# A two-layer trunk: the first stage in a written order with four column groups, two of them summed in SBUF, and the bias of pw2 as products

## The chip, the cores and the metric

The kernel runs on one core of a Trainium2 chip. The metric is the device time of one execution in microseconds; the number given for the kernel before is the median of three runs.

## The reference, cut to what matters

The trunk has two layers on 256 tokens of width 2048, all in float32. Layer 0 mixes tokens by a Conformer convolution, layer 1 by differential attention; both end in a squared-ReLU MLP of width 8192. Each sub-layer is modulated by vectors made from a condition `c`. The change lies in layer 0's mixer:

```python
cond = jax.nn.silu(c)
mod = cond @ ada_w[i] + ada_b[i]                       # [2048] x [2048, 12288]
sh_m, sc_m, g_m, sh_f, sc_f, g_f = jnp.split(mod, 6, axis=-1)
h = x * (1.0 + sc_m) + sh_m
# conformer_conv(h)
u = h @ w1 + b1                                        # pw1: [256, 2048] x [2048, 4096]
a, gt = jnp.split(u, 2, axis=-1)
u = a * sigmoid(gt)
u = depthwise_conv31(u) + b_dw                         # causal, per channel
u = silu(layer_norm(u, g, b))
y = u @ w2 + b2                                        # pw2: [256, 2048] x [2048, 2048]
x = layer_norm(alpha * x + g_m * y, ln_mix_g, ln_mix_b)
h = x * (1.0 + sc_f) + sh_f                            # the MLP follows
```

## The kernel before, in words

**Products.** A float32 product is made of three: weights and activations are each split into a rounded part (hi) and the rest (lo), and hi·hi, hi·lo and lo·hi are added up in PSUM. A weight tile comes by DMA in halves or whole (512 KB to 1 MiB), ACT casts it to hi (L424, later L493), DVE (later sometimes POOL) subtracts to get lo (L426, L494), and PE runs the products, 128 rows of k, 128 tokens and 512 columns each (L440 to L442 in pw1, L526 to L528 in pw2). There are two token tiles.

**Condition vectors.** `cond` is the SiLU of c, made on ACT (L156) and DVE, and copied 32 times for PE (L160). A slice of a modulation vector is made in one of two ways from 1 MiB loads `aw`. `ada_slice_dve_steps`: DVE multiplies each row block by its cond column and sums up (L236), and at the end PE adds over partitions with a vector of ones (L218). `ada_slice_steps`: PE multiplies with the copied cond (L268), ACT copies the row out (L272), PE transposes it (L253), and DVE adds the bias. In names such as `aw_3_8_1` the first number is the vector (0 SH_M, 1 SC_M, 2 G_M, 3 SH_F, 4 SC_F), the second its first block of 128 columns, the third the load; `aacc`, `aps`, `arow` and `apt` are the sums, the PE sums, the row and the columns of such a slice.

**The first stage** (loop at L850 to L880). pw1 has eight column groups of 256 + 256 columns (value and gate). While the shift and scale of the first sub-layer are still coming in, in four slices of 512 features, three groups, 2, 0 and 1 (`FIRST`), are multiplied slice by slice, as far as h is known. Their six accumulators (three groups, two token tiles) take all four banks `mm` and two of the three banks `tp` that transposes use too. Raw ada loads use the two buffers `araw` and, two in three, the four weight buffers `wraw`. In this stage a scheduler that simulates the engines sets the order of each engine's instructions; from its end PE's order is as written.

**The rest of layer 0's mixer.** Groups 3 to 7 follow, 16 k-blocks each at a stretch (`group`, L446). After each pair of k-blocks a tick passes, and work that was put off by a number of ticks (`defer`) is written there: gating (`glu`, L756 to L783: ACT copies the accumulator out, L760; PE transposes, L773 and L774; sigmoid on ACT; product on DVE), then the convolution (`conv_pe`, L712: taps on DVE, L720; twelve shifted copies on ACT, L729, and four on DVE; 64 small products in each of two halves, L738). `pump_conv` starts steps of the list `ada_q` in between, 32 (`ADA_T1`) by the end of pw1: 16 of G_M, 8 of SC_F and 8 of SH_F. At tick 28 the gate vector is broadcast, and POOL multiplies the bias of pw2 with it and adds it to z (`base_bias`, L659 and L663). Then comes `FILL`: 3, 2, 2, 1 and 0 further ada steps around the last two convolution halves, the LayerNorm and the first transposes of SiLU (`sw`). Then pw2 (`out_proj`, `run_jobs`), four column groups of 512, with the remaining ada steps of layer 0 spread over it (`pump_t2`), and the MLP.

**Small rows.** Biases and gains come as rows by DMA on ACT's queue (L127, L153), are transposed by PE and kept as columns. Some are loaded at the start; `ada_b` of layer 1, the MLP's biases, the gain of the attention's norm and six LayerNorm rows are loaded in `other_vectors`, which stands in the third slice of the first stage. Each of these loads has a completion counter of a small set that both SP's and ACT's loads take in turn, and a load that takes a counter again waits for the load that had it.

## Time and profile before

| | us |
|---|---|
| median of three runs | 2433.89 (2429.94 to 2435.54) |
| the profiled execution, its own time | 2432.41 |
| its span in the trace | 2430.6 |
| PE busy, share of the span | 2277.4, 94% |
| DVE, ACT, POOL busy | 1759.5, 1070.6, 264.9 |

Engines: PE multiplies, PEld loads its weights beside that, DVE, ACT and POOL do elementwise work, SP starts transfers; ACTq and SPq are the queues from which ACT and SP start them. Times are microseconds from the start of the span unless a column says ns. A group's row ends with the idle time of its engine just ahead of it and what ended that. In a window's row stand its length, the busy time and count of each engine, the granted TensorE clock (1 is full), the share of time in which the DMA engines were busy, and the rate.

### The profile page before, as it was taken

What the parts mean: (1) busy time and instruction counts of PE and PEld (TensorE: products, weight loads), DVE (VectorE), ACT (ScalarE), POOL (GpSimd) and SP (SyncE); (2) the same over time, 40 slices, a digit from 0 to 9 for tenths busy, and PEclk for the clock granted to TensorE, in tenths of its full rate; (3) what the DMA queues carried; (4) which work ended last, traced back from release to release, by engine and by line L of the source; (5) the groups of instructions that cost most, each with busy time, mean ns of one, the idle gap of its engine ahead of it and who ended that gap; (6) DMA issues with size and microseconds to landing.
All of it is one profiled execution on the core that took longest, in us unless ns stands there. A gap on an engine that the chain in (4) does not pass through costs nothing.

```text
span 2430.6 us, 28467 instructions
## 1 busy us (share of the span) xinstructions
PE 2277.4 (94%) x11119; PEld 1816.0 (75%) x11119; DVE 1759.5 (72%) x1977; ACT 1070.6 (44%) x1391; POOL 264.9 (11%) x174
## 2 busy tenths in 40 slices
PE   4588997989999999999998999998999999999997
PEld 2366664867778888888876888886788888888886
DVE  5588744879798888878868777886867565565566
ACT  2337554444434434434444544443543443443442
POOL 0000011232150000000024200012214000000002
PEclk9789998999999999999999999999999999999999
DMA  9998767658988888888875666685676555556562
GB/s 354 312 331 292 247 220 263 240 209 290 333 309 319 293 322 278 315 314 294 299 254 189 203 237 220 236 291 185 236 277 227 190 186 190 191 185 197 181 223 102
DMA packets 272547, 609.57 MB, mean 251 GB/s; under 512 B 11098, under 2 KB 44448, under 8 KB 259100
## 3 DMA queue, kind: packets, MB, share of 16 engines
q1 hardware_dynamic: 271560, 607.24, 72.2%
q8 instruction: 87, 1.43, 0.2%
q10 hardware_dynamic: 852, 0.51, 0.1%
q14 instruction: 48, 0.39, 0.0%
HBM read 605.58 MB, written 2.13 MB: 250 GB/s over the span
## 4 chain that ended last, share of the span: by engine, by line
PE 75%; DVE 10%; DMA 6%; ACT 4%; issue 3%; POOL 1%; ACTq 0%; DVEq 0%; SPq 0%; POOLq 0%
PE w_ps L527 17%; PE w_ps L526 17%; PE w_ps L528 17%; DMA aw<-in_ada_w_dram 4%; DVE wl_w L494 2%; DVE aacc L236 2%; PE aps L268 1%; PE pw_ps L440 1%; DVE acc L294 1%; PE pw_ps L441 1%; PE qkv_q_ps L528 1%; PE pw_ps L442 1%; PE qkv_v_ps L528 1%; PE qkv_v_ps L526 1%; PE qkv_v_ps L527 1%
## 5 line engine op out<-in xcount | busy, mean ns | idle before, releaser
L494 DVE TENSOR_TENSOR wl_w<-w_w,wh_w 128x1024 fp32r<-128x1024 f32 x502 | 634.3, 1281 | 332.7 <-ACT wh_w L493 332.5
L493 ACT CAST wh_w<-w_w 128x1024 fp32r<-128x1024 f32 x512 | 537.5, 1053 | 754.1 <-PE w_ps L528 579.3
L526 PE MATMUL w_ps<-wh_w,hm_hi 128*128 128x512 f32 x1024 | 403.9, 394 | 4.5 <-ACT hm_hi L361 4.5
L527 PE MATMUL w_ps<-wl_w,u_hi 128*128 128x512 f32 x1024 | 399.0, 390 | 6.3 <-DVE wl_w L494 6.3
L527 PE MATMUL w_ps<-wl_w,hm_hi 128*128 128x512 f32 x1024 | 400.5, 391 | 4.7 <-DVE wl_w L494 4.7
L528 PE MATMUL w_ps<-wh_w,hm_lo 128*128 128x512 f32 x1024 | 400.8, 391 | 1.0 <-DVE hm_lo L364 1.0
L526 PE MATMUL w_ps<-wh_w,u_hi 128*128 128x512 f32 x1024 | 400.0, 391 | 0.0
L528 PE MATMUL w_ps<-wh_w,u_lo 128*128 128x512 f32 x1024 | 398.6, 389 | 0.0
L294 DVE SCALAR_TENSOR_TENSOR acc<-adaw,cond,acc 128x2048 f32<-128x2048 f32 (+1 forms) x105 | 243.0, 2315 | 0.1
L526 PEld LDWEIGHTS w_ps<-wh_w,hm_hi 128*128 128x128 f32 x1024 | 193.2, 189 | 49.2 <-ACT hm_hi L361 6.2
L527 PEld LDWEIGHTS w_ps<-wl_w,u_hi 128*128 128x128 f32 x1024 | 192.3, 188 | 47.9 <-DVE wl_w L494 8.4
L527 PEld LDWEIGHTS w_ps<-wl_w,hm_hi 128*128 128x128 f32 x1024 | 193.5, 189 | 45.1 <-DVE wl_w L494 6.0
L528 PEld LDWEIGHTS w_ps<-wh_w,hm_lo 128*128 128x128 f32 x1024 | 193.2, 189 | 43.0 <-DVE hm_lo L364 2.6
L526 PEld LDWEIGHTS w_ps<-wh_w,u_hi 128*128 128x128 f32 x1024 | 192.3, 188 | 42.0 <-issue 2.5
L528 PEld LDWEIGHTS w_ps<-wh_w,u_lo 128*128 128x128 f32 x1024 | 192.2, 188 | 39.9
L494 POOL TENSOR_TENSOR wl_w<-w_w,wh_w 128x1024 fp32r<-128x1024 f32 x10 | 24.0, 2404 | 1095.7 <-ACT wh_w L493 1095.7
L236 DVE SCALAR_TENSOR_TENSOR aacc<-aw,cond,aacc 128x512 f32<-128x512 f32 (+1 forms) x120 | 128.2, 1069 | 16.0 <-DMA aw<-in_ada_w_dram 14.0
L426 DVE TENSOR_TENSOR wl_pw<-w_pw,wh_pw 128x1024 fp32r<-128x1024 f32 x64 | 79.8, 1260 | 60.5 <-ACT wh_pw L424 60.4
L440 PE MATMUL pw_ps<-wh_pw,h_hi 128*128 128x512 f32 x256 | 106.6, 416 | 6.2 <-ACT h_hi L361 6.2
L441 PE MATMUL pw_ps<-wl_pw,h_hi 128*128 128x512 f32 x256 | 102.7, 401 | 0.0
L442 PE MATMUL pw_ps<-wh_pw,h_lo 128*128 128x512 f32 x256 | 99.1, 396 | 0.0
L424 ACT CAST wh_pw<-w_pw 128x1024 fp32r<-128x1024 f32 x64 | 65.9, 1048 | 68.6 <-PE pw_ps L442 58.7
(322 smaller groups left out, 3189.4 us busy)
## 6 DMA issues: line engine op xcount, KB each, us to landing
w_w<-in_mlp_w_dram SPq DMA_DIRECT2D x256, 1024.0 KB, 5.5
adaw<-in_ada_w_dram SPq DMA_DIRECT2D x96, 1024.0 KB, 6.1
aw<-in_ada_w_dram SPq DMA_DIRECT2D x84, 1024.0 KB, 7.3
w_pw<-in_conv_pw_w_dram SPq DMA_DIRECT2D x64, 512.0 KB, 7.2
w_pw<-in_conv_pw_w_dram SPq DMA_DIRECT2D x16, 1024.0 KB, 5.2
w_qkv_q<-in_attn_qkv_w_dram SPq DMA_DIRECT2D x16, 1024.0 KB, 5.3
w_qkv_k<-in_attn_qkv_w_dram SPq DMA_DIRECT2D x16, 1024.0 KB, 5.1
w_qkv_v<-in_attn_qkv_w_dram SPq DMA_DIRECT2D x16, 1024.0 KB, 5.2
```

What stands on the lines that cost most here:

```text
L236: nc.vector.scalar_tensor_tensor(st["acc"], wv[:, kc % per, :], cond[:, kc:kc + 1], st["acc"], ALU.mult, ALU.add)
L294: nc.vector.scalar_tensor_tensor(st["acc"], w, cond[:, kc:kc + 1], st["acc"], ALU.mult, ALU.add)
L424: nc.scalar.copy(hi, rq)
L426: eng.tensor_tensor(lo, rq, hi.bitcast(F32), op=ALU.subtract)
L440: nc.tensor.matmul(pss[t], lhsT=xh, rhs=wh, start=(kc == 0), stop=False)
L441: nc.tensor.matmul(pss[t], lhsT=xh, rhs=wl, start=False, stop=False)
L442: nc.tensor.matmul(pss[t], lhsT=xl, rhs=wh, start=False, stop=(kc == nk - 1))
L493: nc.scalar.copy(hi, rq)
L494: eng.tensor_tensor(lo, rq, hi.bitcast(F32), op=ALU.subtract)
L526: nc.tensor.matmul(pss[tt], lhsT=xh, rhs=wh, start=(kc == 0), stop=False)
L527: nc.tensor.matmul(pss[tt], lhsT=xh, rhs=wl, start=False, stop=False)
L528: nc.tensor.matmul(pss[tt], lhsT=xl, rhs=wh, start=False, stop=(kc == nk - 1))
```

## The change

1. **Small rows.** The ten row loads of `other_vectors` move to the start of the program, on ACT's queue, ahead of `cond`.
2. **First stage.** Five slices of 2, 4, 4, 4 and 2 blocks of 128 features. Groups 0 and 1 (`RES`) keep their accumulators in PSUM; groups 2 and 3 (`ROT`) are multiplied into `tp` banks slice by slice, and each slice's result is added to sums in SBUF (first copied by ACT, then added by DVE). Four groups are so done by the end of the stage, in place of three. Raw ada loads use the two `araw` buffers and two halves of the buffer of the convolution, so that the four weight buffers hold weights alone. Loads, splits, ada steps and products of PE, DVE, ACT and SP stand in the order in which they are written (`first_part`).
3. **Convolutions.** `conv_pe` is cut into taps, shifts and products, which are put off to ticks of their own (`CONV_AT`); the taps' 64 small copies become 16.
4. **Steps of ada.** The list is cut in two, `dve_q` (G_M, SC_F) and `pe_q` (SH_F). During pw1 24 steps of `dve_q` run and none of `pe_q`; FILL takes eight of `pe_q`, and pw2 the other eight, with eight of `dve_q`. The gate's broadcast moves from tick 28 into FILL.
5. **Bias of pw2.** `base_bias` goes from here. Each accumulator of pw2 begins with two products with four rows of weights (L549 of the new kernel): a selector of the quarter and the bias, hi and lo.

```diff
-FIRST = (2, 0, 1)
-ADA_T1 = 32
+RES = (0, 1)
+ROT = (2, 3)
+SLICES = ((0, 2), (2, 4), (6, 4), (10, 4), (14, 2))
+ADA_T1 = 24
-SLICES = ((0, 4), (4, 4), (8, 4), (12, 4))
-CONV_AT = {2: 1, 0: 4, 1: 7}
+CONV_AT = (3, 7, 11, 15, 19, 23, 28)
...
+    late_rows = {}
+    for n, (name, vs) in enumerate((("adab1", [ada_b[1]]), ("b1", [mlp_b1[0], mlp_b1[1]]), ("subg", [attn_subln_g[0]]),
+                                    ("ln", [ln_mix_g[0], ln_mix_b[0], ln_ffn_g[0], ln_ffn_b[0], ln_mix_g[1],
+                                            ln_mix_b[1]]))):
+        o = 0
+        for v in vs:
+            r = vec_rows(v)
+            nc.scalar.dma_start(vtok[o:o + r.shape[0], 1, n * P:(n + 1) * P], r)
+            o += r.shape[0]
+        late_rows[name] = vtok[:o, 1, n * P:(n + 1) * P]
     cT = as_cols(c_rows, "c")
...
-        if first and n_raw[0] % 3:
-            return wraw.tile([P, 2048], F32, tag="raw", name=name)
+        if first:
+            n_raw[0] += 1
+            if n_raw[0] % 4 in (3, 0):
+                return ux[:, n_raw[0] % 4 // 3 * 2048:(n_raw[0] % 4 // 3 + 1) * 2048]
         return araw.tile([P, 2048], F32, tag="araw", name=name)
...
+                        if kc == 0 and job["bias"] is not None:
+                            for n, (sel, row) in enumerate(job["bias"]()):
+                                nc.tensor.matmul(pss[tt], lhsT=sel, rhs=row, start=(n == 0), stop=False)
...
+    def ada_pair(s):
+        sc_step, sh_step = ada_step[s].pop(0)
+        sc_step()
+        sh_step()
+        for _ in range(2):
+            if ada_load:
+                ada_load.pop(0)()
...
+    for _ in range(4):
+        ada_load.pop(0)()
+    for t in range(NT):
+        nc.sync.dma_start(z[:, t, :], x[0, t * P:(t + 1) * P, :])
+    for _ in range(N_RAW):
+        load_w()
...
+        for n, g in enumerate(order[s]):
+            split_w()
+            pss = pss0[g] if g in RES else [tp_tile(f"pw1_{g}_{s}_ps{t}") for t in range(NT)]
...
+                mm_parts(pss, hT, parts[:nf // 2], f0, k0, k1, False)
+                end_ada(s + 1)
+                mm_parts(pss, hT, parts[nf // 2:], f0 + nf // 2, k0, k1, False)
...
+            if g in ROT:
+                for t in range(NT):
+                    if s == 0:
+                        nc.scalar.copy(accs[g][t], pss[t])
+                    else:
+                        nc.vector.tensor_tensor(accs[g][t], accs[g][t], pss[t], op=ALU.add)
+                cs[g]["ut"] = accs[g]
```

**ACT, the start of the program.** Before, the load of the activation table and the sigmoid of `cond` stand after the rows that the first stage needs at once, and seven others behind them. A wait `DMAHW6` is one for completion counter 6.

```order
L127 DMA rows_conv<-in_conv_ln_b_dram 16x128 [waits DMAHW3_49]
L156 ACT_TABLE_LOAD
L156 ACTIVATE cond<-cols_c 128x16 [waits DVE_49]
L127 DMA rows_adab_635<-in_ada_b_dram 96x128 [waits DMAHW5_49,PE_49]
L127 DMA rows_ln<-in_ln_mix_g_dram 16x128 [waits DMAHW7_49,PE_49]
L127 DMA rows_ln<-in_ln_mix_b_dram 16x128 [waits DMAHW1_49]
L127 DMA rows_ln<-in_ln_ffn_g_dram 16x128 [waits DMAHW2_49]
L127 DMA rows_ln<-in_ln_ffn_b_dram 16x128 [waits DMAHW3_49]
L127 DMA rows_ln<-in_ln_mix_g_dram 16x128 [waits DMAHW4_49]
L127 DMA rows_ln<-in_ln_mix_b_dram 16x128 [waits DMAHW6_49]
```

Now, with the table and the sigmoid on L165:

```order
L160 DMA vtok<-in_ada_b_dram 96x128 [waits DMAHW5_49]
L160 DMA vtok<-in_mlp_b_dram 64x128 [waits DMAHW7_49]
L160 DMA vtok<-in_mlp_b_dram 64x128 [waits DMAHW1_49]
L160 DMA vtok<-in_attn_subln_g_dram 2x128 [waits DMAHW3_49]
L160 DMA vtok<-in_ln_mix_g_dram 16x128 [waits DMAHW5_49]
L160 DMA vtok<-in_ln_mix_b_dram 16x128 [waits DMAHW7_49]
L160 DMA vtok<-in_ln_ffn_g_dram 16x128 [waits DMAHW1_49]
L160 DMA vtok<-in_ln_ffn_b_dram 16x128 [waits DMAHW3_49]
L160 DMA vtok<-in_ln_mix_g_dram 16x128 [waits DMAHW5_49]
L160 DMA vtok<-in_ln_mix_b_dram 16x128 [waits DMAHW6_49]
L165 ACT_TABLE_LOAD
L165 ACTIVATE cond<-cols_c 128x16 [waits DVE_49]
```

The ten loads stand ahead of the sigmoid. The last of them takes a counter of SP's, as the last one before did; counted through, it is that of SP's twelfth load, 7.25 MiB into what SP asks for.

**DVE, the end of the first stage.** `aacc_1_12` is the last scale slice before, `aacc_2_0` the first slice of G_M; the `wl` are splits of pw1 weights, with group and slice in the name (`wl_pw_1_2`).

```order
L236 SCALAR_TENSOR_TENSOR aacc_1_12_828<-aw_1_12_3_845,cond,aacc_1_12_828 128x512 x2
L364 TENSOR_TENSOR h_lo<-h_h_706,h_hi 128x512
L236 SCALAR_TENSOR_TENSOR aacc_1_12_828<-aw_1_12_3_845,cond,aacc_1_12_828 128x512 x2
L383 TENSOR_SCALAR h_h_716<-h_t_711,h_mul,mod_0_132 128x256
L234 TENSOR_SCALAR aacc_2_0_1106<-aw_2_0_0_1104,cond 128x1024
L236 SCALAR_TENSOR_TENSOR aacc_2_0_1106<-aw_2_0_0_1104,cond,aacc_2_0_1106 128x1024
```

Now the last scale slice is `aacc_1_14`, its second load in half of the convolution's buffer (`conv_ux`):

```order
L249 SCALAR_TENSOR_TENSOR aacc_1_14_955<-conv_ux,cond,aacc_1_14_955 128x256
L249 SCALAR_TENSOR_TENSOR aacc_2_0_1269<-aw_2_0_1_1272,cond,aacc_2_0_1269 128x1024
L249 SCALAR_TENSOR_TENSOR aacc_1_14_955<-conv_ux,cond,aacc_1_14_955 128x256
L249 SCALAR_TENSOR_TENSOR aacc_2_0_1269<-aw_2_0_1_1272,cond,aacc_2_0_1269 128x1024
L249 SCALAR_TENSOR_TENSOR aacc_1_14_955<-conv_ux,cond,aacc_1_14_955 128x256 x3
L249 SCALAR_TENSOR_TENSOR aacc_2_0_1269<-aw_2_0_2_1345,cond,aacc_2_0_1269 128x1024
L249 SCALAR_TENSOR_TENSOR aacc_1_14_955<-conv_ux,cond,aacc_1_14_955 128x256
L447 TENSOR_TENSOR wl_pw_1_3_0_1029<-w_pw_1_3_789,wh_pw_1_3_0_1028 128x1024
L447 TENSOR_TENSOR wl_pw_1_3_1_1033<-w_pw_1_3_789,wh_pw_1_3_1_1032 128x1024
L934 TENSOR_TENSOR vtok<-vtok,pw_3_3_ps_1039 128x512
L934 TENSOR_TENSOR vtok<-vtok,pw_3_3_ps_1040 128x512
L447 TENSOR_TENSOR wl_pw_0_4_0_1068<-w_pw_0_4_840,wh_pw_0_4_0_1067 128x1024
```

Sums of G_M stood behind the last scale sum and now stand between its parts; splits of the fourth slice and the PSUM adds stand behind both.

**PE, around the start of pw2.** `aps_3` are SH_F steps, `cv` and `vt` the last convolutions, `sw` the transposes ahead of SiLU, `pw_0_ps` the first accumulators of pw2.

```order
L738 MATMUL cv_2993<-conv_x,conv_w_1_1_2891 32x256 x16
L268 MATMUL aps_3_12_2981<-aw_3_12_1_3028,condr 32x512 x4
L704 MATMUL vt_3034<-ident,vpe_3026 128x128 x2
L268 MATMUL aps_3_12_2981<-aw_3_12_2_3040,condr 32x512 x4
L268 MATMUL aps_3_12_2981<-aw_3_12_3_3062,condr 32x512 x4
L934 MATMUL sw_3072<-ident,vtok 128x128 x4
L934 MATMUL sw_3082<-ident,vtok 128x128 x4
L934 MATMUL sw_3092<-ident,vtok 128x128 x4
L526 MATMUL pw_0_ps_3112<-wh_pw_0_0_0_3116,swish_hi 128x512
L527 MATMUL pw_0_ps_3112<-wl_pw_0_0_0_3117,swish_hi 128x512
```

Now:

```order
L1031 MATMUL sw_3008<-ident,vtok 128x128 x4
L1031 MATMUL sw_3018<-ident,vtok 128x128 x4
L1031 MATMUL sw_3028<-ident,vtok 128x128 x4
L283 MATMUL aps_3_8_3067<-aw_3_8_0_3065,condr 32x512 x4
L549 MATMUL pw_0_ps_3048<-pw2b_hl,one_2680 128x512 x2
L550 MATMUL pw_0_ps_3048<-wh_pw_0_0_0_3052,swish_hi 128x512
L552 MATMUL pw_0_ps_3048<-wl_pw_0_0_0_3053,swish_hi 128x512
L553 MATMUL pw_0_ps_3048<-wh_pw_0_0_0_3052,swish_lo 128x512
L549 MATMUL pw_0_ps_3049<-pw2b_hl,one_2680 128x512 x2
```

All SH_F steps stood ahead of the first product of pw2; now the first step of its third slice (`aps_3_8`) stands just ahead of it, the other seven of the last two slices stand between products of pw2, and the two bias products open each accumulator.

421 lines of the change are left out of this document (234 added, 187 removed).

## The prediction

> **What bounds the kernel now.** I read the page first, for the whole.
>
> ```profile
> span 2430.6 us, 28467 instructions
> PE 2277.4 (94%) x11119; PEld 1816.0 (75%) x11119; DVE 1759.5 (72%) x1977; ACT 1070.6 (44%) x1391; POOL 264.9 (11%) x174
> PE 75%; DVE 10%; DMA 6%; ACT 4%; issue 3%; POOL 1%; ACTq 0%; DVEq 0%; SPq 0%; POOLq 0%
> ```
>
> PE is busy for 94% of the span and holds 75% of the chain that ended last. The change touches the program up to the end of pw2, so I cut that part into four stretches by the PE rows and asked for the busy time of each engine in them: A, the first stage with three column groups (0 to 185.3); B, the other five groups (to 388.3); C, the last convolutions and the LayerNorm (to 420.6); D, pw2 (to 517.5). Three shorter windows follow. Columns: length, busy time of PE, PEld, DVE, ACT and POOL, granted clock, DMA share, GB/s.
>
> ```profile
> 0.00:185.30 185.30, 115.84 (x523) 77.14 (x523) 116.19 (x197) 57.67 (x100) 1.98 (x11) 0.84 0.96 333
> 185.30:388.30 203.00, 190.45 (x1576) 133.60 (x1574) 133.16 (x182) 119.22 (x179) 17.48 (x12) 0.98 0.73 253
> 388.30:420.60 32.30, 22.32 (x214) 9.17 (x212) 11.25 (x27) 14.89 (x26) 0.72 (x1) 0.84 0.75 261
> 420.60:517.50 96.90, 94.60 (x424) 77.91 (x424) 76.97 (x74) 42.35 (x50) 23.60 (x9) 0.96 0.73 252
> 25.00:50.00 25.00, 14.19 (x54) 6.41 (x47) 9.64 (x14) 8.94 (x13) 0.00 (x0) 0.86 1.07 372
> 100.00:125.00 25.00, 23.33 (x104) 16.58 (x102) 10.51 (x13) 10.31 (x13) 0.00 (x0) 0.84 0.77 250
> 411.70:418.50 6.80, 6.09 (x27) 2.70 (x28) 2.44 (x6) 4.47 (x6) 0.06 (x1) 0.50 0.75 261
> ```
>
> A is bound by transfers: the DMA engines are busy for 0.96 of it, PE for 116 of 185 us. B and D are bound by PE (190 of 203, 95 of 97). So work that moves from B into A's idle PE time is a gain, if A doesn't get longer by as much. Two of the groups on PE up to 192 us say the same, with their idle time and its releaser at the end:
>
> ```profile
> L268 PE MATMUL aps<-aw,condr 128*32 128x512 f32 x128 | 24.9, 887 | 27.0 <-DMA aw<-in_ada_w_dram 27.0
> L218 PE MATMUL apt<-ones,aacc 128*128 128x1 f32 x32 | 4.9, 269 | 14.4 <-DVE aacc L236 14.4
> ```
>
> PE waits 27.0 us for ada weights, and 14.4 us for the DVE sums made from them.
>
> **Stretch A, its start.** The ACT timeline of the first 28 us (start, duration):
>
> ```profile
> 8.14 1.28 ACT L156 ACT_TABLE_LOAD   x1 [8.14 <-DMA rows_adab<-in_ada_b_dram]
> 9.44 0.22 ACT L156 ACTIVATE cond<-cols_c 128x16 f32<-128x16 f32 x1
> 26.09 0.32 ACTq L127 DMA_DIRECT2D rows_ln<-in_ln_mix_b_dram  x1
> 26.44 1.28 ACT L905 ACT_TABLE_LOAD   x1 [16.78 <-DMA z<-in_x_dram]
> ```
>
> The DVE timeline has the copy of cond for PE, behind which the ada steps start:
>
> ```profile
> 9.95 0.42 DVE L160 COPY condr<-cond 128x512 f32<-128x512 f32 x1
> ```
>
> cond is ready at 9.66 now, and both its forms 0.71 later, at 10.37. The last row load goes out only at 26.09, though it is small: the queue's completion counters are shared with SP's loads, and the order lists for it a wait on counter 6, whose earlier user lands then (the page puts the wait of the next ACT instruction down to z). About 7 MiB had been asked for ahead of it. In the new order ten row loads stand ahead of cond, and the last of them waits on counter 6 as well, for SP's twelfth load, which ends 7.25 MiB into the stream. I put it at 27, and both forms of cond at 27 + 0.32 + 1.28 + 0.22 + 0.71 = 29.5 in place of 10.4. The Trainium skill (DMA: Bandwidth & Descriptors, Issuing engines are not separate DMA queues) says that DMAs started by several engines end on the same 16 DMA engines, and that only the sequencer's time to initiate is at stake, usually a small one. By that, ten loads would cost ACT ten issues, cond would come near 14, and A would be about 5 us shorter than I say; the trace disagrees, as the row at 26.09 is an issue of 0.32 us that stood until then.
>
> What a late cond costs is small, since the loads run on until their buffers are full: 4 MiB of ada weights, 2 of x, four weight tiles of 0.5, 8 MiB, full at about 28. The first ada steps give buffers back from 31.5 (PE) to 33.5 (DVE, whose step has eight sums at 0.476, below). So transfers stand still for some 5 us, and resume at 33.5.
>
> **A, its transfers.** From there 40 MiB remain to the last ada load: 32 of ada, 2 of x and 14 of weights make 48, less the 8. One MiB (1.049 MB) takes 2.82 us at the 372 GB/s of the window 25 to 50, and 3.02 at 333 / 0.96 = 347, A's rate while busy. With 2.95, the last ada load lands at 33.5 + 118 = 151.5. In the trace of before (a row below) the last ada step of A starts at 157.6, with one group fewer.
>
> **A, its tail.** DVE and ACT rows by shape (up to 440 us) for this and the rest, then the landing time of a load on a light queue, the last number of its row:
>
> ```profile
> L236 DVE SCALAR_TENSOR_TENSOR aacc<-aw,cond,aacc 128x1024 f32<-128x1024 f32 x48 | 61.4, 1280 | 10.7 <-DMA aw<-in_ada_w_dram 10.3
> L426 DVE TENSOR_TENSOR wl_pw<-w_pw,wh_pw 128x1024 fp32r<-128x1024 f32 x64 | 79.8, 1260 | 60.5 <-ACT wh_pw L424 60.4
> L671 DVE TENSOR_TENSOR pw_g<-pw_ps,gb 128x512 f32<-128x512 f32 x7 | 4.8, 680 | 2.7 <-PE pw_ps L528 2.7
> L783 DVE SCALAR_TENSOR_TENSOR u<-pa,cols_conv,sg 128x256 f32<-128x256 f32 x10 | 4.3, 476 | 2.2 <-ACT sg L781 2.2
> L383 DVE TENSOR_SCALAR h_h<-h_t,h_mul,mod 128x256 f32<-128x256 f32 x8 | 4.2, 538 | 2.6 <-PE h_t L377 2.6
> ```
>
> ```profile
> L729 ACT COPY conv_x<-u 32x568 f32<-32x568 f32 x56 | 37.2, 664 | 8.7 <-DVE u L783 8.0
> L361 ACT CAST h_hi<-h_h 128x512 fp32r<-128x512 f32 x8 | 4.8, 618 | 0.2
> ```
>
> ```profile
> w_w<-in_mlp_w_dram SPq DMA_DIRECT2D x256, 1024.0 KB, 5.5
> ```
>
> In DVE's new order the sums of G_M, a vector that nobody needs before FILL, alternate with those of the last scale slice, up to the third G_M load, which needs the buffer of the first. So the last scale sum waits for: two G_M loads still queued, 2 x 2.95 = 5.9; the step on the first, 2.9; the third load from issue to landing, 5.5; its step and a sum of 0.48, together 1.7: 16.0. (A price of 0 is the other end: R1.) Then, in DVE's order, two splits 2 x 1.26, two PSUM adds 2 x 0.68 (by L671, the row that reads PSUM and SBUF at this width), a split 1.26, three G_M sums of 1.28, small ones 0.7, the h scaling 0.54 and the cast 0.62: 10.8, say 11. The last slice's products come next; PE's timeline gives their pace, and the last ada step of A:
>
> ```profile
> 60.06 0.39 PE L440 MATMUL pw_ps<-wh_pw,h_hi 128*128 128x512 f32 x1
> ...
> 62.78 0.39 PE L440 MATMUL pw_ps<-wh_pw,h_hi 128*128 128x512 f32 x1
> ...
> 157.55 1.06 PE L268 MATMUL aps<-aw,condr 128*32 128x512 f32 x8
> ```
>
> Twelve products go by in 62.78 - 60.06 = 2.72 us, 0.227 each; 48 take 11. The splits of the third and fourth group stand behind four more G_M sums, 5.1. A ends at 151.5 + 16 + 11 + 11 + 5 = 194.5, with four groups done.
>
> Hidden in A: the fourteen other PSUM adds (9.5 us of DVE), the narrower scale sums (32 of 0.476), one more group's eight splits (10.1); DVE has 69 us idle there, and would have to run out of them to cost anything. The 48 wct copies fewer are worth nothing for the same reason.
>
> **Stretch B.** The PE timeline, at the places that the rest needs:
>
> ```profile
> 194.30 0.47 PE L773 MATMUL pa<-ident,utok 128*128 128x128 f32 x1 [6.29 <-ACT utok L760]
> ...
> 346.38 1.06 PE L268 MATMUL aps<-aw,condr 128*32 128x512 f32 x8
> ...
> 394.62 1.93 PE L268 MATMUL aps<-aw,condr 128*32 128x512 f32 x8 [4.34 <-DMA aw<-in_ada_w_dram]
> ...
> 411.61 1.92 PE L268 MATMUL aps<-aw,condr 128*32 128x512 f32 x8 [2.71 <-DMA aw<-in_ada_w_dram]
> ```
>
> It loses one group, 96 products of 0.227 = 21.8, and eight SH_F steps of 1.06 = 8.5, which go to D. Of its idle time the 6.29 behind the first stage goes, since the first groups' gating now lies in A between products. What is late next is the first convolution: its twelve ACT copies (0.664 each, 8.0 us) cover about three ticks of products at 2.72, and I leave 2.3 for it, so -4; the ends are -6.3 and 8.0 - 6.3 = +1.7. B = 203.0 - 21.8 - 8.5 - 4 = 168.7.
>
> **Stretch C.** The gate broadcast, with its write and read, comes into FILL, and its transfers stand in SP's queue with the ada loads there, which already wait 4.34 and 2.71. I take +2, between 0 and one landing, 5.5: C = 34.3.
>
> **Stretch D.** It gains the eight SH_F steps, 8.5, and 16 bias products (two for each of four quarters and two token tiles). No row has a product with 4 rows of weights; the nearest is the 0.227 above, so 3.6, between 0 if they fall into a wait for a load, and 16 x 0.39 = 6.2 by the duration of a single one. D moves 252 GB/s x 96.9 us = 24.4 MB, and 8.4 more make 32.8 in some 110 us, 298 GB/s, against the 347 to 372 that A reaches. Most of the loads will be in time; I take 3 us of waits. D = 96.9 + 8.5 + 3.6 + 3 = 112.
>
> Taken out of D's neighbourhood are POOL's bias instructions:
>
> ```profile
> L663 POOL TENSOR_TENSOR z<-z,base_b 128x512 f32<-128x512 f32 x8 | 11.9, 1511 | 0.3
> L659 POOL TENSOR_TENSOR base_b<-base_b,gb 128x512 f32<-128x512 f32 x4 | 5.6, 1390 | 351.8 <-DMA gb<-gb_d 336.8 <-DMA base_b<-in_conv_pw_b_dram 15.0
> ```
>
> 17.5 us, all beside PE work of B, and worth 0: none of the PE waits that I saw in B and C is put down to POOL.
>
> **The sum.** 194.5 + 168.7 + 34.3 + 112 = 509.5 in place of 517.5: -8, and nothing behind it changes. The profiled execution took 2432.41 us, so 2424.4; the median of the runs shown, 2433.89, is 1.5 above it: 2426.
>
> **The rivals.** *R1, the G_M sums don't hold the last slice* (its loads are there in time, because SP sends them while DVE is late): the 16.0 falls to the 1.7 of the last step, A ends near 180, and the time is 2426 - 14 = 2412. For it: L218 waits for DVE only 14.4 us in all of A now. Against: two buffers for these loads, and the third load can't be sent before the first is used. 0.20.
>
> *R2, slower: pw2 waits for each moved SH_F step.* These steps stand between pw2's products, and PE takes them in order, so a load that is late stops the products behind it. Their two buffers also serve SC_F's DVE steps. The two FILL rows above show 2.71 and 4.34 for such a wait; eight of them are 22 to 35 us in place of 3, so 2445 to 2458, 2451 in the middle. It ends slower than before from 8 + 3 + 5 = 16 us, 2.0 per step. Against: D has a third of its DMA time free. The window at 411.7 shows clock 0.50 right behind a wait of 2.71, and its steps take 1.92 in place of 1.06; that could come on top. The Trainium skill (TensorE: Matmul & The Clock Gate, HAM oscillation — how this bites in real kernels) puts the limit at idle gaps of over about 3.4 us; the trace disagrees, as 2.71 is the wait just ahead of that window, and by the rule only the longer of the waits would cost clock. 0.17.
>
> *R3, no change: transfers of A run worse than 2.95 per MiB*, as in the window 100 to 125 (250 GB/s, 4.2 per MiB while it lasts). At 3.15, A's mean of 333 GB/s, the 40 MiB take 8 us more and the time is 2434; the change then only moves work. For it: more small transfers and a written order with no slack. 0.20. The forecast keeps 0.43.
>
> **How the numbers follow.** What a measurement of this kernel can tell from no change is about 0.2%, 4.9 us. The forecast is 8 us faster, with some 5 to either side by the ends above: 0.32 of its 0.43 is faster, 0.11 the same. R1 is faster, 0.20. R3 is the same, 0.14, or slower, 0.06. R2 is slower, 0.17. Together faster 0.52, same 0.25, slower 0.23. The range goes from 2406 (R1 with B's full -6.3 and no stalls in D) to 2443 (R3 with C and the bias at their upper ends); outside are most of R2 and the tail of R1.
>
> **What would show it right or wrong.** Right: cond on ACT near 27 to 29; the last ada product of the first stage near 151; the last scale sums waiting for an aw load near 155 to 165; the first product of the fifth group near 195; the first pw2 product near 397 and its last near 509; no L659 or L663 of old on POOL. A fifth group that starts at 180 is R1; SH_F rows in pw2 with 2 us or more behind an aw load are R2; a last ada product near 160 is R3. The whole working is wrong if B shortens by much less than 30: then PE was not its bound, and ACT, with 119 us of copies and casts there, was.

## The result and the profile after

The changed kernel takes 2447.25 us (median of four runs, 2444.53 to 2452.89), the kernel before 2432.47 beside it: a ratio of 1.0063, with a 95% interval of 1.0041 to 1.0085. It is slower by some 15 us, where 8 us faster was forecast and 2443 was the upper end of the range. The profiled execution took 2444.53.

The page of the changed kernel, span and engines:

```profile
span 2442.7 us, 28548 instructions
PE 2288.3 (94%) x11167; PEld 1815.8 (74%) x11167; DVE 1760.1 (72%) x1986; ACT 1068.5 (44%) x1374; POOL 246.9 (10%) x162
```

The four stretches, then three short windows of the first stage (length, busy time of PE, PEld, DVE, ACT and POOL, clock, DMA share, GB/s):

```profile
0.00:210.30 210.30, 138.59 (x652) 95.71 (x653) 134.75 (x212) 70.06 (x102) 1.98 (x11) 0.92 0.93 317
210.30:380.20 169.90, 159.53 (x1393) 111.34 (x1395) 120.95 (x171) 103.52 (x157) 0.00 (x0) 0.97 0.63 211
380.20:418.37 38.17, 26.25 (x239) 11.26 (x238) 15.03 (x33) 17.19 (x31) 0.72 (x1) 0.78 0.73 254
418.37:529.60 111.23, 111.14 (x508) 81.19 (x504) 66.82 (x73) 41.21 (x48) 22.46 (x9) 0.97 0.83 293
30.00:34.00 4.00, 3.05 (x32) 1.38 (x32) 3.49 (x9) 1.79 (x5) 0.00 (x0) 1.00 0.08 24
113.00:121.00 8.00, 7.41 (x38) 4.47 (x38) 2.48 (x6) 6.31 (x14) 0.00 (x0) 1.00 0.48 157
157.00:167.00 10.00, 10.00 (x52) 7.46 (x51) 7.93 (x14) 2.10 (x2) 0.00 (x0) 0.91 0.60 194
```

pw2 ends at 529.6 where it ended at 517.5, and these 12.1 us are the whole difference of the spans. The transfers of the first stage stand still at 30 to 34, and move less than half of their rate at 113 to 121.

From PE's timeline I take, for every run, the first product of the group behind the first stage (end of A), the last GLU transpose (end of B), the first and the last product of pw2 (ends of C and D). By this count the borders of before are 184.2, 388.4, 420.6 and 517.5. Length of each in us:

| run | A | B | C | D | pw2 ends |
|---|---|---|---|---|---|
| before | 184.2 | 204.2 | 32.2 | 96.9 | 517.5 |
| forecast | 194.5 | 168.7 | 34.3 | 112 | 509.5 |
| changed | 210.2 | 170.0 | 38.2 | 111.3 | 529.6 |
| e1_rows_behind | 207.2 | 167.8 | 37.9 | 111.2 | 524.2 |
| e2_gm_held | 198.6 | 175.0 | 37.5 | 111.8 | 523.0 |
| e3_old_bias | 210.5 | 170.0 | 37.6 | 112.5 | 530.5 |
| e5_vectors_mid | 210.7 | 173.1 | 37.3 | 111.7 | 532.7 |
| e6_free_order | 201.7 | 181.7 | 37.0 | 111.6 | 532.0 |
| e8_bias_once | 209.0 | 171.7 | 37.8 | 110.0 | 528.5 |
| c3_rows_gm_shf | 197.1 | 192.0 | 30.4 | 101.6 | 521.0 |
| c4_rows_gm | 195.0 | 174.4 | 37.2 | 111.9 | 518.5 |
| c5_three | 184.2 | 201.5 | 37.4 | 112.0 | 535.1 |
| c6_last_early | 196.5 | 171.6 | 37.6 | 112.2 | 517.9 |
| c7_all | 196.5 | 174.5 | 36.0 | 109.5 | 516.6 |
| b1_bias | 183.1 | 205.5 | 31.3 | 104.4 | 524.3 |
| b2_shf | 182.1 | 189.6 | 34.4 | 102.4 | 508.5 |
| b3_rows | 190.5 | 202.5 | 32.0 | 94.5 | 519.5 |

What lies behind pw2 is the same code in all of them, and took 1912.6 to 1919.9 us in these single executions. Each row of the table is one execution too. So I read the place of an effect from this table and its size in time from the ratios, which rest on 4 to 10 runs each.

The start of the first stage, on ACT's timeline of the changed kernel:

```profile
28.37 0.32 ACTq L160 DMA_DIRECT2D vtok<-in_ln_mix_b_dram  x1
28.72 1.28 ACT L165 ACT_TABLE_LOAD   x1 [28.72 <-DMA w_pw<-in_conv_pw_w_dram]
30.01 0.21 ACT L165 ACTIVATE cond<-cols_c 128x16 f32<-128x16 f32 x1
```

The tenth row load waits for the weight load that had its counter, and the sigmoid of cond ends at 30.2. The end of the ada loads, first as issues of SP with their landing time, then as the last two shift steps on PE, then the first product of the fifth group:

```profile
L217 SPq DMA_DIRECT2D conv_ux<-in_ada_w_dram x2: 1363/2115/2867, 144.8 to 146.3; - x2
DMA to landing us min/median/max: 10.3/10.3/10.3
```

```profile
161.78 1.07 PE L283 MATMUL aps<-aw,condr 128*32 128x256 f32 x16
...
168.49 1.07 PE L283 MATMUL aps<-conv_ux,condr 128*32 128x256 f32 x16
...
210.22 0.40 PE L461 MATMUL pw_ps<-wh_pw,h_hi 128*128 128x512 f32 x1
```

The last loads are in by about 157 (146.3 + 10.3), and neither step waits for one: they stand behind products, and PE is busy for all of 157 to 167. DVE's groups between 167 and 199:

```profile
L249 DVE SCALAR_TENSOR_TENSOR aacc<-aw,cond,aacc 128x1024 f32<-128x1024 f32 x11 | 14.0, 1277 | 0.6 <-DMA aw<-in_ada_w_dram 0.5
L447 DVE TENSOR_TENSOR wl_pw<-w_pw,wh_pw 128x1024 fp32r<-128x1024 f32 x5 | 6.0, 1218 | 0.3 <-ACT wh_pw L446 0.3
L249 DVE SCALAR_TENSOR_TENSOR aacc<-conv_ux,cond,aacc 128x256 f32<-128x256 f32 x7 | 3.4, 481 | 0.1
```

Eleven sums of G_M take 14.0 us in the tail, and the five splits that PE needs 6.0. From the last shift step to the end of the stage DVE is the fuller of the two engines (35.4 of 40.6 us, PE 30.9), and PE waits for it. The window, two of PE's waits between 157 and 210.3 (us in total, times, longest), then the last scale sum and the first product of the last slice:

```profile
169.60:210.20 40.60, 30.94 (x122) 23.63 (x123) 35.36 (x50) 21.21 (x31) 0.00 (x0) 0.87 0.90 311
```

```profile
PE pw_ps L462 <- DVE wl_pw L447: 4.1, 2, 2.5
PE pg L801 <- DVE vtok L934: 2.8, 1, 2.8
```

```profile
176.31 0.48 DVE L249 SCALAR_TENSOR_TENSOR aacc<-conv_ux,cond,aacc 128x256 f32<-128x256 f32 x1
```

```profile
187.50 0.50 PE L461 MATMUL pw_ps<-wh_pw,h_hi 128*128 128x512 f32 x1 [1.29 <-ACT h_hi L374]
```

Last, PE's groups in C (380.2 to 418.4) and in D:

```profile
L283 PE MATMUL aps<-aw,condr 128*32 128x512 f32 x72 | 12.2, 755 | 11.9 <-DMA aw<-in_ada_w_dram 11.5 <-ACT arow L287 0.4
```

```profile
L283 PE MATMUL aps<-aw,condr 128*32 128x512 f32 x60 | 8.6, 635 | 0.1
L549 PE MATMUL pw_ps<-pw2b_hl,one 4*128 4x512 f32 x16 | 6.8, 507 | 0.0
```

Nine SH_F steps lie in C and wait 11.5 us for their loads, four of them by these amounts: 2.43 (its row is in the last section), then

```profile
403.21 1.07 PE L283 MATMUL aps<-aw,condr 128*32 128x512 f32 x8 [1.55 <-DMA aw<-in_ada_w_dram]
406.44 1.93 PE L283 MATMUL aps<-aw,condr 128*32 128x512 f32 x8 [2.16 <-DMA aw<-in_ada_w_dram]
...
416.50 1.93 PE L283 MATMUL aps<-aw,condr 128*32 128x512 f32 x8 [5.38 <-DMA aw<-in_ada_w_dram]
```

The first three waits, 6.1, are of FILL's eight steps. The ninth step, at 416.50, is `aps_3_8`, the first of the eight that moved; it stands just ahead of the first product of pw2. The other seven, between the products of pw2, wait 0.1.

### The profile page after: what moved, and what is told of

Read it like the earlier page. It is cut to its first block, busy times and chain, and to the rows that moved or that the text cites. A ratio compares the mean times of both kernels' runs of the same rounds, so it can differ in the third digit from the quotient of the medians.

```text
span 2442.7 us, 28548 instructions
## 1 busy us (share of the span) xinstructions
PE 2288.3 (94%) x11167; PEld 1815.8 (74%) x11167; DVE 1760.1 (72%) x1986; ACT 1068.5 (44%) x1374; POOL 246.9 (10%) x162
## 4 chain that ended last, share of the span: by engine, by line
PE 74%; DVE 9%; DMA 5%; ACT 4%; issue 3%; POOL 1%; ACTq 0%; DVEq 0%; POOLq 0%; SPq 0%
PE w_ps L550 17%; PE w_ps L553 17%; PE w_ps L552 17%; DMA aw<-in_ada_w_dram 2%; DVE wl_w L515 2%; PE cv L767 2%; DMA w_w<-in_mlp_w_dram 2%; PE qkv_q_ps L553 1%; PE qkv_q_ps L552 1%; PE qkv_q_ps L550 1%; PE qkv_v_ps L553 1%; PE qkv_v_ps L550 1%; PE qkv_v_ps L552 1%; PE qkv_k_ps L553 1%; PE qkv_k_ps L550 1%
## 5 line engine op out<-in xcount | busy, mean ns | idle before, releaser
L249 DVE SCALAR_TENSOR_TENSOR aacc<-aw,cond,aacc 128x1024 f32<-128x1024 f32 (+2 forms) x95 | 99.4, 1046 | 11.2 <-DMA aw<-in_ada_w_dram 9.2
L463 PE MATMUL pw_ps<-wh_pw,h_lo 128*128 128x512 f32 x256 | 104.4, 408 | 0.0
L447 DVE TENSOR_TENSOR wl_pw<-w_pw,wh_pw 128x1024 fp32r<-128x1024 f32 x64 | 76.8, 1220 | 37.2 <-ACT wh_pw L446 37.1
L283 PE MATMUL aps<-aw,condr 128*32 128x512 f32 (+1 forms) x240 | 37.4, 713 | 52.6 <-DMA aw<-in_ada_w_dram 29.5
```

The costliest lines, as they stand in the source:

```text
L249: nc.vector.scalar_tensor_tensor(st["acc"], wv[:, kc % per, :], cond[:, kc:kc + 1], st["acc"], ALU.mult, ALU.add)
L447: nc.vector.tensor_tensor(lo, rq, hi.bitcast(F32), op=ALU.subtract)
L463: nc.tensor.matmul(pss[t], lhsT=xl, rhs=wh, start=False, stop=(kc == last))
```

## The experiments

My theory after the result: the written order lets the transfers of A stand still and puts G_M's sums into its tail, while C and D cost about what was forecast. The rivals are written with each run. A ratio is to the kernel before, as run on the same chip; the changed kernel's is 1.0063.

**e1_rows_behind.** The loop of the row loads, moved as a whole:

```diff
-    late_rows = {}
-    ...
     cT = as_cols(c_rows, "c")
...
     nc.vector.tensor_tensor(cond, cond, cT, op=ALU.mult)
+    late_rows = {}
+    ...
```

> The ten row loads stand behind the sigmoid of cond again, all else as in the changed kernel. Theory (the time of the first stage was lost where the written order lets the transfers stand still, at 30 to 34 us, at 113 to 121 and at 157 to 167, and where sums of G_M stand in its tail): cond is ready near 10 in place of 30.4, the window 30 to 34 moves 300 GB/s or more in place of 24, and the time falls by 4 to 6 us against the changed kernel. Rival (the loss lies in pw2, by the SH_F steps and the bias products, and the later holes swallow an earlier start): within 2 us of the changed kernel.

Measured: 2444.58, ratio 1.0051 (1.0036 to 1.0066); pw2 ends 5.4 earlier. The sigmoid runs at 9.82, and the window 30 to 34 moves 274 GB/s, somewhat under the theory's 300. The one profiled execution shows the theory's 4 to 6; the time moved by about 3, and the intervals overlap, so the times alone don't show a gain.

**e2_gm_held.**

```diff
-            nc.sync.dma_start(tv, av[:, per * a:per * (a + 1), n0:n0 + w])
+            with tc.issue_after(raws["dma"].ins) if v == G_M else ExitStack():
+                nc.sync.dma_start(tv, av[:, per * a:per * (a + 1), n0:n0 + w])
```

> The loads of G_M are held until SP has issued the weight load that was written just before each (the fifth group's first for the first of them), so no sum of G_M stands between the last scale sums. Theory: DVE has about eleven sums of 1.28 us fewer between 167 and 195, and about 17 us of G_M transfers leave that stretch; the fifth group starts 10 to 15 us earlier than 210.2, and the time falls by 9 to 14 us against the changed kernel. Rival (the last weight loads are waited for anyway): at most 3 us.

Measured: 2439.56, ratio 1.0032 (1.0021 to 1.0043), the largest gain of one edit in the changed kernel. DVE's groups of this run, 167 to 199:

```profile
L448 DVE TENSOR_TENSOR wl_pw<-w_pw,wh_pw 128x1024 fp32r<-128x1024 f32 x9 | 11.0, 1221 | 2.3 <-ACT wh_pw L447 2.3
L250 DVE SCALAR_TENSOR_TENSOR aacc<-aw,cond,aacc 128x1024 f32<-128x1024 f32 x4 | 5.1, 1284 | 0.1
```

Four sums of G_M in place of eleven, nine splits in place of five: A ends 11.6 earlier, though the last ada step stands where it stood (its end is at 170.3, in the changed kernel 169.6). The last scale sum ends at 169.6 in place of 176.8, so the sums of G_M had held it by some 7 us. B takes 5.0 of the 11.6 back, as the sums now lie there. So the theory holds for A, and the time fell by about 7.5, under its 9 to 14.

**e3_old_bias.**

```diff
-    defer(29, pw2_bias)
...
     gate0["gb"] = gate_bcast(mods[(0, G_M)], "gb0")
+    base_bias(gate0["gb"], conv_pw2_b[0], "base0", 2)
...
-             bias=lambda q: lambda: [(bias0["one"][:, q:q + 1].broadcast_to([4, P]), bias0["hl"][:, n, :])
-                                     for n in range(2)])
```

> The bias of pw2 goes onto z through POOL again, right behind the gate's broadcast; no bias products. Theory: the 16 products go, 16 x 0.227 = 3.6 us at full clock and up to 6.8 as they ran, so -4 to -7 against the changed kernel; POOL's 17.5 us lie beside pw2. Rival: POOL's adds now stand ahead of the gated adds to z at the end of pw2's first quarter and hold the accumulators: 0 to +5.

Measured: 2446.57, ratio 1.0057 (1.0036 to 1.0078): no gain to speak of, though the 16 products are gone. SH_F on PE in D, in this run:

```profile
L283 PE MATMUL aps<-aw,condr 128*32 128x512 f32 x60 | 9.5, 697 | 7.0 <-DMA aw<-in_ada_w_dram 7.0
```

PE has no wait for POOL in D, so my rival was wrong in its mechanism, though no gain is what it forecast. SP issues POOL's broadcasts at the same time as pw2's loads, and the SH_F steps now wait 7.0 us for theirs, in place of 0.1; that the one makes the other is likely and not shown by itself. So this run does not price the products, as it brings a cost of its own; b1 does.

**e5_vectors_mid.**

```diff
+            if n == 2 and s == CV_AT:
+                conv_vectors()
+            if n == 2 and s == OV_AT:
+                other_vectors()
             split_w()
...
-        if s == CV_AT:
-            conv_vectors()
-        if s == OV_AT:
-            other_vectors()
```

> The column vectors of the convolution and the other vectors are made in the middle of their slices of the first stage, not at the end. Theory: twelve tap copies of 4.7 us on ACT no longer stand between two slices, the stop of the transfers at 113 to 121 shrinks by some 5 us, and the time falls by 3 to 6 us against the changed kernel. Rival (the stop moves with the copies, or comes from buffers that are full at each border of slices whatever ACT does): within 2 us.

Measured: 2450.12, ratio 1.0073 (1.0055 to 1.0091); A the same, B 3.1 longer. The stop moved with the copies (two windows of this run):

```profile
105.00:110.00 5.00, 3.18 (x15) 2.36 (x15) 4.89 (x7) 2.52 (x4) 0.00 (x0) 1.00 0.56 182
113.00:121.00 8.00, 7.90 (x26) 6.49 (x27) 4.88 (x10) 4.37 (x6) 0.00 (x0) 0.66 0.87 303
```

As the rival has it, the stop only moved; the time rose by some 2 by the ratios, with overlapping intervals, and did not fall. The last ada step ends at 165.0, 4.5 earlier than in the changed kernel, and A ends no earlier: in this kernel the end of A does not hang on that step.

**b1_bias, b2_shf, b3_rows** make one part of the change each in the kernel before. b1 takes the change's own lines for the bias (its part 5); b3 those for the rows (part 1). b2:

```diff
-ADA_T1 = 32
+ADA_T1 = 24
-    for f0 in range(0, KC, 4):
-        ada_q.extend(ada_slice_steps(0, SH_F, f0, 4, m_shf))
-    ada_q.extend(ada_slice_dve_steps(0, SC_F, 8, 8, m_scf, False))
+    shf = [st for f0 in range(0, KC, 4) for st in ada_slice_steps(0, SH_F, f0, 4, m_shf)]
+    ada_q.extend(shf[:8])
+    for pair in zip(ada_slice_dve_steps(0, SC_F, 8, 8, m_scf, False), shf[8:]):
+        ada_q.extend(pair)
```

> The kernel before with one part of the change alone: the bias of pw2 as 16 products; POOL's bias work and its four broadcasts are gone. Theory (the products lie on PE's path in pw2 and POOL's work lay on nobody's): pw2 takes 3.6 us more at full clock and up to 6.8 as the products ran in the changed kernel, +3 to +7 against before. Rival (the broadcasts and POOL's adds held something in the stretch before): 0 or faster.

> The kernel before with one part of the change alone: 24 steps of ada in pw1 in place of 32, eight SH_F steps in FILL and the other eight between the products of pw2, one SC_F step ahead of each. Theory (PE bounds both stretches, the loads are mostly in time): 185 to 388 us gets about 8.5 shorter, pw2 about 8.5 longer, with 0 to 6 us of waits for loads: 0 to +6 against before. Rival (each moved step waits for its load by 2 us or more): +16 or more.

> The kernel before with one part of the change alone: the ten row loads at the start of the program, ahead of cond. Theory: cond comes near 27 to 30 in place of 9.7, the transfers stop for some 5 us, and the time rises by 3 to 6 us. Rival (the first stage takes it back at a later wait): within 1.5 us.

b1: 2440.04, ratio 1.0049 (1.0033 to 1.0065). D is 7.5 longer, pw2 ends 6.7 later, as the theory had it; the time rose by more, about 12, and why isn't shown. The products in this run:

```profile
L528 PE MATMUL pw_ps<-pw2b_hl,one 4*128 4x512 f32 x16 | 6.3, 472 | 0.0
```

b2: 2426.04, ratio 0.9986 (0.9976 to 0.9996). Theory and rival were both too dark: the move of the eight SH_F steps is a gain, of some 3 us in the time (1 to 6 by the interval) and of 9.0 at the end of pw2 in the profiled execution. B, C and D of b2:

```profile
182.10:371.70 189.60, 179.48 (x1498) 130.11 (x1500) 135.33 (x178) 118.94 (x179) 18.82 (x12) 0.98 0.68 230
371.70:406.10 34.40, 24.53 (x237) 10.77 (x236) 14.99 (x32) 16.42 (x29) 0.72 (x1) 0.88 0.80 271
406.10:508.50 102.40, 102.40 (x493) 78.69 (x491) 74.08 (x75) 42.24 (x51) 21.49 (x9) 0.99 0.86 312
```

B got 14.6 shorter for 8.5 us of steps, D only 5.5 longer, and PE in D is never idle.

b3: 2438.10, ratio 1.0029 (1.0019 to 1.0039), about 7 us slower, a little over the theory's 3 to 6. The sigmoid and the transfers around it:

```profile
30.75 0.22 ACT L166 ACTIVATE cond<-cols_c 128x16 f32<-128x16 f32 x1
```

```profile
26.00:32.00 6.00, 0.31 (x4) 0.20 (x8) 0.97 (x3) 2.52 (x3) 0.00 (x0) 1.00 0.23 81
```

A ends 6.3 later; B, C and D are each a little shorter, and pw2 ends only 2.0 later in this execution.

**e6_free_order.**

```diff
-    first_part = tc.manual_schedule(engines={engines.PE, engines.DVE, engines.Activation, engines.SP})
+    first_part = tc.manual_schedule(engines={engines.PE})
```

> The changed kernel, but only PE's order is as written in the first stage; DVE's, ACT's and SP's is the scheduler's again, with the same four groups, slices and buffers. Theory (the written order makes the transfers stand still between slices): the last ada step ends at least 8 us ahead of 169.6, and the time falls by 5 to 12 us against the changed kernel. Rival (the last ada load is late because 3.5 MiB of the fourth group's weights, some 10 us, stand ahead of it, in whatever order): the last ada step within 4 us of 169.6, the time within 4 us.

Measured: 2449.36, ratio 1.0088 (1.0069 to 1.0107). The stop is gone and A is busier with transfers (windows of this run):

```profile
113.00:121.00 8.00, 6.38 (x22) 4.52 (x21) 6.72 (x12) 7.78 (x18) 0.00 (x0) 0.79 1.07 372
...
0.00:201.70 201.70, 137.80 (x644) 97.22 (x645) 131.72 (x210) 65.44 (x92) 1.98 (x11) 0.88 0.98 334
```

A is 8.5 shorter, but the last ada step still ends at 169.1 and B is 11.7 longer, so nothing is won. My theory of the written order falls in its first form: filling the stop does not bring the last step forward. The last step is where the rival had it; the time is some 6 over the changed kernel's by the ratios, with overlapping intervals, and c5 below speaks against the rival's reason. Why B got longer, these runs do not settle.

**c3_rows_gm_shf, c4_rows_gm, c5_three.** c4 is e1 and e2 together. c3 has eight SH_F steps in pw1 besides; c5 has three groups in the written order:

```diff
+        while 16 - len(pe_q) < 8 * n_conv[0] / (4 * (8 - len(RES + ROT))):
+            pump_early(pe_q)
```

```diff
-ROT = (2, 3)
+ROT = (2,)
-CONV_AT = (3, 7, 11, 15, 19, 23, 28)
+CONV_AT = (3, 7, 11, 15, 23, 31, 36)
...
-    order = [tuple(g for gs in zip(ROT, RES) for g in gs)] * (len(SLICES) - 1) + [RES + ROT]
+    order = [ROT + RES] * (len(SLICES) - 1) + [RES + ROT]
...
+        per_n = len(nxt) // 2
...
-                for _ in range(2 if n == 0 and len(nxt) > 2 else 1):
+                for _ in range(per_n):
```

> The changed kernel with three of its parts undone: the row loads behind cond, the G_M loads held until the weight load written before each, and eight SH_F steps in pw1 again. If the parts add up (-2.7 and -7.7 measured for the first two, about 0 for the third, whose 8.5 us move from pw2 back to the stretch before): about 2437, within 3 us. Rival (the SH_F steps cost waits and clock in FILL and pw2 beyond their own time): 2433 or less.

> The changed kernel with the row loads behind cond and the G_M loads held. If the two parts add up as they ran alone (-2.7 and -7.7): about 2437, within 3 us. Rival (the later holes swallow the earlier start once the tail is short): no better than 2439.6, the run with the G_M loads held alone.

> As the run with rows behind cond and G_M held, but the written first stage does three column groups (2, 0, 1; group 2 summed in SBUF), and group 3 follows with the others; the convolutions' ticks move by up to 8. Theory (a group in the first stage costs its transfers, 3.5 MiB or some 10 to 12 us ahead of the last ada step, and saves 96 products of 0.227, 21.8 us, behind it): 8 to 11 us slower than the run with four groups. Rival (PE in the first stage runs at a lower clock and in the written order waits with the transfers, so a group there is worth nothing): within 3 us.

c4: 2437.78, ratio 1.0028 (1.0016 to 1.0040); pw2 ends 11.1 earlier than changed, where e1 and e2 alone gave 5.4 and 6.6. At the end of pw2 the parts nearly add up; by the ratios c4 is only 1 us under e2, so the times don't exclude the rival. c3: 2438.71, ratio 1.0040 (1.0024 to 1.0056). Against c4 its B is 17.6 longer, its C and D 6.8 and 10.3 shorter: the steps cost twice their time in B, as in b2. But pw2 ends only 2.5 later than in c4, where the same steps made 9.0 between before and b2, and the time is some 3 us longer, with overlapping intervals: the price of these steps depends on the kernel around them. c5: 2447.09, ratio 1.0062 (1.0046 to 1.0078), 9 us slower than c4, as the theory had it: A 10.8 shorter, B 27.1 longer. So the fourth group does pay for itself within the written order. (The ticks of the later convolutions move too, which the run doesn't take apart.) But the reason that the theory gave for A's part does not hold. With 3 MiB of weights fewer ahead of it, the last ada load lands at 153.2 (141.5 + 11.7) in place of c4's 154.0 (143.8 + 10.2), and the last step stands at the same place, first c5, then c4:

```profile
165.60 1.07 PE L284 MATMUL aps<-conv_ux,condr 128*32 128x256 f32 x16
```

```profile
165.58 1.07 PE L284 MATMUL aps<-conv_ux,condr 128*32 128x256 f32 x16
```

The 10.8 us lie behind that step, where the fourth group's products and splits are missing, and not in the transfers ahead of it.

**e8_bias_once.** One product of 36 rows for two of 4:

```diff
-             bias=lambda q: lambda: [(bias0["one"][:, q:q + 1].broadcast_to([4, P]), bias0["hl"][:, n, :])
-                                     for n in range(2)])
+             bias=lambda q: lambda: [(bias0["one"][:, q:q + 1].broadcast_to([36, P]), bias0["hl"])])
```

> The changed kernel with the bias of pw2 as one product for each accumulator, with 36 rows of weights (hi in rows 0 to 3, lo in rows 32 to 35, zeros between), so 8 in place of 16. Theory (a product of 512 columns costs the same for any number of rows, 0.43 as these ran): -3.4 us, pw2 108 in place of 111.3. Rival (the cost is the start of an accumulator or the clock at pw2's start): within 1.5 us.

Measured: 2445.78, ratio 1.0052 (1.0035 to 1.0069); D 1.3 shorter. PE's group in D of this run, and one product with the next:

```profile
L549 PE MATMUL pw_ps<-pw2b_hl,one 36*128 36x512 f32 x8 | 4.5, 568 | 0.0
```

```profile
450.37 0.50 PE L549 MATMUL pw_ps<-pw2b_hl,one 36*128 36x512 f32 x1
450.80 0.50 PE L550 MATMUL pw_ps<-wh_pw,swish_hi 128*128 128x512 f32 x1
```

Half the products took 4.5 us in place of 6.8. From its start to the next product the one takes 0.43, where the pair in the changed kernel takes 0.65 (its rows are in the last section). So 0.22 is saved for each accumulator, some 1.8 us in all, and not the theory's 3.4: the one product costs two thirds of the two. The rival's size fits D here (against c6, c7 has a D 2.7 shorter); that the cost is the start of an accumulator isn't shown.

**c6_last_early, c7_all.** In the changed kernel 12 us lie between the last landing, at about 157, and the start of the last step. c6 is c4 with the last slice's steps one group earlier; c7 adds e8's edit.

```diff
-                for _ in range(2 if n == 0 and len(nxt) > 2 else 1):
+                for _ in range(2 if n == 0 else 1):
```

> As the run with rows behind cond and G_M held, and the last slice's two shift steps and scale steps both stand behind the first column group of the fourth slice, not behind its first and second. Their loads have landed by about 158, and the last step ran at 166.7. Theory (the written order, which lets the last ada step wait for a whole group's products, is what made the first stage 11 us longer than its transfers): the last step moves to about 160, the fifth group starts 4 to 7 us earlier than 195.0, and the time falls by 4 to 7 us. Rival (PE is busy without a gap from 134 to 185 in that run, so its products only change places): the fifth group starts within 2 us of 195.0.

> As the run above, with the bias as one product of 36 rows for each accumulator as well. If the parts add up (-1.5 measured for it alone): within 3 us of the run above less 1.5, and no faster than the kernel before. Rival: faster than before.

c6: 2435.06, ratio 1.0014 (1.0000 to 1.0028). The last step ends at 162.5, not 166.7, and A ends at 196.5, not 195.0: the rival holds (the time is some 3 under c4's by the ratios, with overlapping intervals). The window 134 to 185 of c4 shows why:

```profile
134.00:185.00 51.00, 49.14 (x252) 38.28 (x251) 34.84 (x61) 18.51 (x25) 0.00 (x0) 0.96 0.75 249
```

PE is busy for 49.1 of 51 us, so from 134 on the first stage of c4 is bound by PE, and no longer by transfers. (In the changed kernel, with the sums of G_M in the tail, PE is busy for 46.0 of the same 51.) c7: 2433.08, ratio 1.0008 (0.9995 to 1.0021): with its mended parts the changed kernel is as fast as before, and not faster. The fastest of all is b2, the kernel before with eight SH_F steps moved.

## Why the prediction was wrong, point by point

**Wrong: A, "With 2.95, the last ada load lands at 33.5 + 118 = 151.5", and the tail put right behind it.** A ended at 210.2 in place of 194.5, 15.7 later. Against the marks of the sum:

| from, to | forecast | measured |
|---|---|---|
| start to the last ada landing | 151.5 | 156.6 |
| to the end of the last scale sum | 16 | 20.2 |
| to the last slice's first product | 11 | 10.7 |
| to the end of A | 16 | 22.7 |

The first row is the transfers: the sum had one stop of them, at the start, and the trace shows a second at 113 to 121; the 40 MiB took 3.09 us per MiB from 33.0 on.

The second and the last row are the step that failed, the path. The sum let everything wait for the last landing and counted 48 products behind it, as if PE and DVE had caught up by then. They hadn't. DVE took up the first of the last scale sums only at 164.8, 8 us after the landing. PE was full from the landing until 175, with the fourth slice's products ahead of the last step, and behind that step 96 products of pw1 were left, not 48. Among them stood the gating of the first groups, which the sum put at nothing: in the last row PE waits 1.7 for a split, 2.8 for an addition to the sums in SBUF, and 1.4 for sigmoids.

So the end of A doesn't follow the last ada step: e5 (against the changed kernel) and c6 (against c4) moved the step forward by 4.5 and 4.2, and A ended no earlier; e2 and c5 (against the same two) made A 11.6 and 10.8 shorter with the step in its place. I read A's 0.96 DMA share and PE's 116 of 185 us as one state. With the sums of G_M held, PE is what bounds the end of the stage (c4, 49.1 of 51 us); with them in the tail, as in the changed kernel, DVE is the fuller engine from 170 on.

**Right in kind, too large: G_M in the tail.** The sum has 16.0 for the hold of the last scale sum, which measured some 7 (e2), and 3.8 and 5.1 for G_M sums behind it, together 25. Without them A was 11.6 shorter, of which B took 5.0 back. R1, which priced the absence of the hold at 14, didn't happen.

**Right: the late cond.** Both forms of cond were forecast for 29.5 and came at 30.9, the sigmoid ended at 30.2; e1 and b3 price the move at some 3 and 7 us; e1's interval overlaps the changed kernel's, b3's lies clear of 1. By the rule of the Trainium skill that I weighed against this row (DMA: Bandwidth & Descriptors, Issuing engines are not separate DMA queues) cond would have come near 14; the trace goes against it, with the sigmoid's end at 30.2 in the changed kernel and 31.0 in b3.

**Right in sum, partly for wrong reasons: B.** 168.7 forecast, 170.0 measured. The SH_F steps took more than 8.5 with them (14.6 between before and b2, 17.6 between c3 and c4), so the rest of the change, the fourth group with it, brought less than 21.8 and 4. PE's waits in B went from those for the GLU copies to others for the convolutions, 6.5 behind ACT's sigmoids and 2.6 behind `vpe`:

```profile
PE cv L767 <- ACT sg L808: 6.5, 2, 3.7
PE vt L728 <- ACT vpe L771: 2.6, 2, 1.9
```

The convolutions at ticks of their own (part 3 of the change) were never undone, so their share is open. There is a hint that it is a cost: c5, with five groups and no SH_F steps in B, has a B of 201.5, 12 longer than b2's 189.6 with the same; the held sums of G_M may be some 5 of that (e2).

**Too small: C.** 34.3 forecast, 38.2 measured. I priced the gate's transfers alone. FILL's own steps wait 6.1 us for loads, no more than before (4.34 + 2.71 + 0.70). What is new is the first moved step, which stands just ahead of pw2, and waits 5.38 and takes 1.93. In c3, where no step stands there, C is 30.4, with 6.2 of waits in FILL and the gate's broadcast in it as well.

**Right: D, with its terms off.** 112 forecast, 111.3 measured. The 16 products took 6.8, above the 6.2 that was the upper bound and not the 3.6 that I took; the waits of 3 were 0.1. R2, a moved step that holds pw2 until its load is in, came true for one of the eight, the one in C: seven waited for nothing.

**R3** is nearest to what came, with 3.09 us per MiB against its 3.15, but its price of 8 is half of A's error, and neither it nor another rival had the filled engines at the end of A. So the sign was lost in A: 15.7 of the 20.1 us by which pw2 ended later than forecast. Taken apart at pw2's end, rows and G_M are 11.1 of the 12.1 us against before (c4), the bias 6.7 (b1), the moved SH_F steps -9.0 by b2 and -2.5 by c3. That leaves 3 us or -3, by which of the two is taken, for the four written groups and the convolutions' ticks, where I had counted on a gain. Why that gain is missing stays open; no run undoes the convolutions, and c5 shows the fourth group alone as worth 9 us.

## What to carry to other kernels

A stage that is bound by transfers on average can be bound by other engines at its end; before moving work into it, take the windows of its last third and ask what backlog those engines carry there when the last load is in. A step whose load is late holds what stands behind it, so look first at the steps just ahead of a long row of products. Small loads put ahead of everything can wait for large ones through shared completion counters, and hold the instruction behind them. A change of several parts is worth taking apart: here one of them alone beats the kernel before by some 3 us, and two that were priced at a few us cost more than it brought. Prices found in one kernel need not hold in another.

## What the runs showed of the hardware that was not expected

A step whose wait was only 2.43 us ran at half clock, in C of the changed kernel:

```profile
386.51 1.94 PE L283 MATMUL aps<-aw,condr 128*32 128x512 f32 x8 [2.43 <-DMA aw<-in_ada_w_dram]
```

The same step takes 1.06 at full clock, and the one just before it, at 383.01, did. In the rows of C above a step behind a wait of 1.55 took 1.07, and one behind 2.16 took 1.93. These waits are below the gap of about 3.4 us that the Trainium skill gives (TensorE: Matmul & The Clock Gate, HAM oscillation — how this bites in real kernels), as with the 2.71 of the prediction; what else has a part in it, earlier waits for one, isn't shown. A product with 4 rows of weights was no cheaper here than one with 128: a pair of them took 0.65 us from its start to the next product at full clock (450.19 to 450.84), 0.33 each, where a usual product takes 0.227. The one with 36 rows took 0.43 (e8).

```profile
450.19 0.72 PE L549 MATMUL pw_ps<-pw2b_hl,one 4*128 4x512 f32 x2
450.84 0.50 PE L550 MATMUL pw_ps<-wh_pw,swish_hi 128*128 128x512 f32 x1
```
